# The 64 sample rows' projections and the gate rows computed on two column groups of the array

## The chip, the cores and the metric

The kernel runs on one Trainium2 chip, on all 8 cores, each with its own share of the batch. A core has a matrix engine (PE, the TensorE), a vector engine (DVE), a scalar engine (ACT), a general engine (POOL), a queue engine (SP) and 16 DMA engines. The time is that of the slowest of the 8 cores, in device microseconds (us). "Span" is what the profile gives for one core, from its first to its last instruction; the time is some 1.6 us more than the longest span (1.5 to 1.7). A run is in a fast state or in a slow one, in which one die (cores 0 to 3, or 4 to 7) runs at a lower clock.

## The reference

One trunk layer. Each core has one prompt of 2048 tokens and 16 samples of 4 tokens, 64 sample rows in all, so 17 tiles of rows: 16 of 128 tokens, and tile 16 with the samples.

```python
mod = (silu(c) @ w_ada + b_ada)[:, None, :]
sh1, sc1, gt1, sh2, sc2, gt2 = split(mod, 6)            # shift, scale, gate, twice
h    = rmsnorm(x, g_pre_mix) * (1 + sc1) + sh1
proj = h @ w_in
mix  = concat([pool_mixer(...), conv_mixer(...)]) @ w_out     # "output projection"
x    = x + gt1 * rmsnorm(mix, g_post_mix)
h2   = rmsnorm(x, g_pre_ffn) * (1 + sc2) + sh2
up   = h2 @ ffn_w_up
a, b = split(causal_dwconv(concat([ffn_buf, up]), ffn_conv_w), 2)
f    = (silu(a) * b) @ ffn_w_down                              # "down projection"
x    = x + gt2 * rmsnorm(f, g_post_ffn)
# outputs: x, and the last rows of the pooling, convolution and FFN inputs
```

The model width is 1024 (`D`), the FFN width 2816. A gate (`gt1`, `gt2`) is one row for the prompt and one for each of the 16 samples.

## The kernel before

The program lists operations; a planner orders them on the engines by a simulated schedule and draws each dependency as a semaphore. So a change in one place can move the order of loads and of PE everywhere.

The gate rows are products with the stationary operand `REP`, the conditioning with each sample's column repeated for its 4 tokens, plus one for the prompt: 65 columns, one product for each half of the channels. They go through a DRAM scratch to be spread over partitions:

```python
def gate_rows(n, hb):                       # n: first or second gate, hb: half of the channels
    ib, ig = (0, 1) if n == 0 else (4, 5)   # buffers; BIG[4] is "big_79" in the profile
    ...
    mm(PSF[0:65, b, :], [(REP[:, kc, :], W[:, kc, :]) for kc in range(KC)], ..., 512)
    tt(rb[0:65, sl], PSF[0:65, b, :], rb[0:65, sl], ALU.add, ...)       # + bias
    tt(rb[0:65, sl], rb[0:65, sl], rg[0:65, sl], ALU.mult, ...)         # * post-norm weight
    if hb == 1:
        store(gsc_d[n], rb[0:65, :], [r_big[ib]], ...)                  # to the scratch
def gate_load(n):
    # GTS[0:64, :] <- rows of the samples; GTP <- the prompt's row, to 128 partitions
```

The output and down projections of a tile fill a pair of PSUM banks, one for each half of the channels; then the tail normalizes, gates and adds.

```python
def o_mm(t):                                # d_mm(t) is alike, with 22 products a half instead of 8
    b = tail_a(t, x_d, ())                  # takes a bank pair, loads x
    for hb in range(2):
        mm(PSF[0:rows, b + hb, :], [(BY[:, kc, r0:r0 + rows], WO[hb][:, kc, :]) for kc in range(KC)], ..., 512)
def tail_b(t, k, add_eng, parts=1):
    m = turn(tmps)                          # temporary; the first one is BIG[4]
    stats(ps, ...)                          # Square with sum into BIG[m] (as scrap), sqrt, reciprocal
    stt(BIG[m], ps, rstd, gt, mult, mult)   # * 1/rms * gate
    give(b, b + 1)                          # the banks are free
    tt(BIG[xi], BIG[m], BIG[xi], add)       # + x, then the store of y
```

For tile 16 only 64 of the 128 stationary columns are used.

## Time and profile before

| | us |
|---|---|
| time, median of fast runs | 744.4 (744.08 to 744.72) |
| spans of the 8 cores | 740.4 to 742.2 |
| PE busy, slowest core | 691.0 |
| gate rows, 4 groups of 8 products | 6.9 |
| samples' output projection, 16 products | 3.5 |
| samples' down projection, 44 products | 9.6 |
| end of PE to end of span, mean of cores | 5.9 |

From the page of the kernel before, the span, and the line of busy time (us, share of the span, instructions):

```profile
span 742.2 us, 12030 instructions; the slowest of 8 cores (740.4 to 742.2 us)
...
PE 691.0 (93%) x3925; PEld 332.7 (45%) x4000; DVE 469.2 (63%) x624; ACT 328.1 (44%) x576; POOL 271.4 (37%) x293
```

From here on, a line of a timeline has start, duration, engine, line of the kernel, operation, output and inputs, shapes and count; brackets at its end give how long the engine had been idle and what released it. The timeline of PE before, core 2, two of the four gate products:

```profile
164.44 1.89 PE L468 MATMUL ps<-ring_70,rep_46 128*65 128x512 bf16 x8
...
177.27 1.89 PE L468 MATMUL ps<-wg_73,rep_46 128*65 128x512 bf16 x8
```

Eight matmuls of 512 columns take 1.73 us from start to start, with 65 stationary columns as with 128. The timeline before, core 0, ACT at the first two output tiles:

```profile
192.92 1.02 ACT L489 ACTIVATE big_79<-ps 128x1024 bf16<-128x1024 f32 x1 [2.97 <-PE ps L468]
...
196.32 1.02 ACT L489 ACTIVATE big_80<-ps 128x1024 bf16<-128x1024 f32 x1 [1.90 <-PE ps L468]
```

The timeline before, core 2, the end of the kernel:

```profile
726.64 1.02 ACT L489 ACTIVATE big_80<-ps 64x1024 bf16<-64x1024 f32 x1 [8.06 <-PE ps L468]
726.65 9.44 PE L468 MATMUL ps<-wdn_134,g_135 128*128 128x512 bf16 x43 [0.16 <-issue]
...
729.95 1.22 DVE L497 TENSOR_TENSOR big_78<-big_80,big_78 64x1024 f32<-64x1024 f32 x1 [0.17 <-DVE big_80 L493]
...
736.19 0.60 ACT L489 ACTIVATE big_80<-ps 128x512 f32<-128x512 f32 x1 [4.01 <-PE ps L468]
```

The samples' tail (726.6 to 731.2) is hidden under the last tile's matmuls. After PE's end at 736.1 there is only the last tile's second half.

### The profile page before, as it was taken

To read this page: it belongs to the slowest core of one execution; us is meant where nothing else is said; L and a number is where in the kernel's file an instruction comes from. 1 tells how busy PE (TensorE), PEld (TensorE's weight loads), DVE (VectorE), ACT (ScalarE), POOL (GpSimd) and SP (SyncE) were. 2 spreads that over 40 slices of the span, in tenths; PEclk is the share of its full clock that TensorE was granted. 3 is DMA by queue.
4 is the path that set the end of the run, shared out by engine and by line. 5 is a ranking of instruction groups with operands and counts; after the bars stand their busy time and mean duration, and the time that the engine had idled before them with its cause. 6 is when DMAs were issued, how large, how long until landed. Compare 5 with 4: busy or idle time off the path is not lost.

```text
span 742.2 us, 12030 instructions; the slowest of 8 cores (740.4 to 742.2 us)
## 1 busy us (share of the span) xinstructions
PE 691.0 (93%) x3925; PEld 332.7 (45%) x4000; DVE 469.2 (63%) x624; ACT 328.1 (44%) x576; POOL 271.4 (37%) x293
## 2 busy tenths in 40 slices
PE   1588889999999999999999999999999999999996
PEld 1244435544455444444444444445444444444442
DVE  2348688745478889997777511128877777767213
ACT  4526754433477784454454311134444444423111
POOL 2313332232488653434444232223433342322320
PEclk9969999999999999999999999999999999999999
DMA  8999999599868554346989974113335433062422
GB/s 207 187 202 216 204 176 188 102 189 200 229 229 268 202 118 82 57 72 101 149 151 151 208 228 166 57 57 57 59 64 88 76 58 57 1 232 86 137 77 72
DMA packets 25713, 101.33 MB, mean 137 GB/s; under 512 B 3310, under 2 KB 5102, under 8 KB 21812
## 3 DMA queue, kind: packets, MB, share of 16 engines
q0 software_dynamic: 10944, 47.85, 39.8%
q1 hardware_dynamic: 14708, 52.71, 21.6%
q8 instruction: 33, 0.54, 0.3%
q14 instruction: 28, 0.23, 0.1%
HBM read 127.49 MB, written 20.90 MB: 200 GB/s over the span
## 4 chain that ended last, share of the span: by engine, by line
PE 84%; DVE 5%; issue 5%; DMA 3%; ACT 1%; POOL 1%; DVEq 0%; SPq 0%; ACTq 0%; POOLq 0%
PE ps L468 81%; PE ps L695 2%; DMA wsc_2_85<-w_sc 2%; PE ps L476 2%; DMA big_77<-x 1%; DVE big_75 L493 1%; DVE big_79 L493 1%; POOL big_77 L497 0%; DVE ta_107 L493 0%; DVE big_80 L493 0%; DVE ah_81 L502 0%; DVE ah_81 L504 0%; ACT ah_81 L489 0%; DVE by_82 L493 0%; DVE xn_99 L502 0%
## 5 line engine op out<-in xcount | busy, mean ns | idle before, releaser
L468 PE MATMUL ps<-wdn_134,g_135 128*128 128x512 bf16 (+1 forms) x733 | 161.4, 379 | 0.9 <-issue 0.2
L468 PE MATMUL ps<-ah_81,ring_71 128*128 128x512 bf16 (+2 forms) x766 | 148.5, 346 | 5.6 <-DVE ah_81 L502 2.2
L468 PE MATMUL ps<-ah_81,ring_72 128*128 128x512 bf16 (+2 forms) x798 | 148.4, 338 | 2.2 <-DVE big_75 L493 1.1
L468 PE MATMUL ps<-ah_81,ring_70 128*128 128x512 bf16 (+2 forms) x739 | 138.0, 339 | 3.2 <-DVE ah_81 L502 0.9
L468 PEld LDWEIGHTS ps<-wdn_134,g_135 128*128 128x128 bf16 (+1 forms) x748 | 73.3, 99 | 87.1 <-issue 0.8
L468 PEld LDWEIGHTS ps<-ah_81,ring_71 128*128 128x128 bf16 x784 | 67.8, 98 | 80.5 <-issue 6.8
L468 PEld LDWEIGHTS ps<-ah_81,ring_72 128*128 128x128 bf16 x816 | 68.8, 98 | 76.8 <-issue 2.4
L468 PEld LDWEIGHTS ps<-ah_81,ring_70 128*128 128x128 bf16 x752 | 63.6, 98 | 72.0 <-issue 3.6
L586 DVE RECIPROCAL stat_55<-stat_55 128x1 f32<-128x1 f32 (+1 forms) x67 | 10.6, 158 | 121.0 <-ACT stat_55 L489 120.7
L497 POOL TENSOR_TENSOR g_135<-big_75,big_76 128x1024 bf16<-128x1024 f32 x15 | 35.4, 2361 | 65.9 <-DVE big_76 L497 34.4
L497 POOL TENSOR_TENSOR g_135<-big_77,big_78 128x1024 bf16<-128x1024 f32 x15 | 35.4, 2357 | 58.0 <-DVE big_78 L497 32.7
L497 POOL TENSOR_TENSOR g_135<-big_79,big_80 128x1024 bf16<-128x1024 f32 x14 | 33.4, 2383 | 55.3 <-DVE big_80 L497 27.5
L489 ACT ACTIVATE big_80<-ps 128x1024 bf16<-128x1024 f32 (+2 forms) x16 | 15.5, 969 | 73.6 <-PE ps L468 72.7
L493 DVE SCALAR_TENSOR_TENSOR big_75<-ps,vecs_43,big_75 128x1023 f32<-128x1023 f32 (+1 forms) x30 | 38.4, 1278 | 11.8 <-ACT halob_58 L489 4.9
L493 DVE SCALAR_TENSOR_TENSOR big_77<-ps,vecs_43,big_77 128x1023 f32<-128x1023 f32 (+1 forms) x30 | 38.4, 1280 | 11.0 <-ACT halob_58 L489 6.2
L493 DVE SCALAR_TENSOR_TENSOR big_78<-ps,vecs_43,big_78 128x1023 f32<-128x1023 f32 (+1 forms) x30 | 38.4, 1279 | 10.4 <-ACT halo_57 L489 5.0
L493 DVE SCALAR_TENSOR_TENSOR big_76<-ps,vecs_43,big_76 128x1023 f32<-128x1023 f32 (+1 forms) x30 | 38.4, 1279 | 9.3 <-ACT halob_58 L489 4.4
L493 DVE SCALAR_TENSOR_TENSOR big_79<-ps,vecs_43,big_79 128x1023 f32<-128x1023 f32 (+1 forms) x28 | 35.8, 1280 | 12.3 <-ACT halob_58 L489 7.6
L493 DVE SCALAR_TENSOR_TENSOR big_80<-ps,vecs_43,big_80 128x1023 f32<-128x1023 f32 (+1 forms) x28 | 35.8, 1279 | 7.9 <-ACT halob_58 L489 3.6
L489 ACT ACTIVATE big_79<-ps 128x1024 bf16<-128x1024 f32 x14 | 14.3, 1023 | 55.8 <-PE ps L468 54.8
L497 POOL TENSOR_TENSOR big_75<-big_79,big_75 128x256 f32<-128x256 f32 (+1 forms) x16 | 20.0, 1250 | 49.6 <-DVE big_79 L493 30.9
L468 PE MATMUL ps<-wo_138,by_82 128*128 128x512 bf16 (+1 forms) x134 | 31.9, 379 | 0.1
(316 smaller groups left out, 895.2 us busy)
## 6 DMA issues: line engine op xcount, KB each, us to landing
ring_70<-w_up POOLq DMA_DIRECT2D x8, 1024.0 KB, 10.2
ring_71<-w_up POOLq DMA_DIRECT2D x7, 1024.0 KB, 10.9
ring_72<-w_up POOLq DMA_DIRECT2D x7, 1024.0 KB, 10.0
wdn_134<-w_down POOLq DMA_DIRECT2D x11, 512.0 KB, 13.9
y<-big_75 SPq DMA_DIRECT2D x7, 512.0 KB, 3.0
y<-big_76 SPq DMA_DIRECT2D x7, 512.0 KB, 2.6
y<-big_77 SPq DMA_DIRECT2D x7, 512.0 KB, 3.7
big_76<-x SPq DMA_DIRECT2D x6, 512.0 KB, 8.7
```

The source lines that it names most:

```text
L468: inst = e.matmul(bank_ap, l, r, start=(first and i == 0), stop=(last and i == len(pairs) - 1))
L476: inst = e.transpose(o, i, ident)
L489: return K.op("act", lambda e: e.activation(out=out, in_=in_, func=func, **kw), reads=reads, writes=writes, cost=c_act(n, ptr))
L493: return K.op(eng, lambda e: e.scalar_tensor_tensor(out, in0, s, in1, op0, op1), reads=reads, writes=writes, cost=c_dve(n))
L497: return K.op(eng, lambda e: e.tensor_tensor(out, in0, in1, op), reads=reads, writes=writes, cost=c_dve(n) if eng == "dve" else c_pool(n))
L586: K.op("dve", lambda e: e.reciprocal(STAT[0:rows, k + 1, t:t + 1], STAT[0:rows, k + 1, t:t + 1]), reads=[r_stat[k + 1][t]], writes=[r_stat ...
L695: inst = e.matmul(PSF[:, start_b[g, c], :], WINP[:, kc, g * 128:(g + 1) * 128], AH[:, kc, c * 512:(c + 1) * 512], start=(kc == 0), stop=(k ...
```

## The change

With 64 columns or fewer in the stationary operand, two products can use two halves of the array's columns: here the two halves of the channels. The samples' tile then has its channels folded over 128 partitions (64 rows times two halves of 512), so its vector work is half as long. The price: a row's sum of squares lies in two partitions, and a small fp32 matmul with a pairing matrix adds the two. The gate rows use 32 stationary columns (16 samples, prompt, padding), once for both halves.

```diff
+    def mm2(outs, ls, rs, reads, writes, n):
+        def fn(e):
+            for i in range(len(ls)):
+                for o, r in zip(outs, rs[i]):
+                    inst = e.matmul(o, ls[i], r, start=(i == 0), stop=(i == len(ls) - 1))
+    def stats2(src, k, reads, junk, junk_regs):
+        act(junk, src, AF.Square, ..., accum=STAT[:, k, 16:17])
+        mm(PSF[:, b, 0:1], [(PAIR, STAT[:, k, 16:17])], ...)            # adds the halves
+        act(STAT[:, k + 1, 16:17], PSF[:, b, 0:1], AF.Sqrt, ...)        # then reciprocal
-    def gate_rows(n, hb):
+    def gate_rows(n):                       # both halves at once
+        mm2([PSF[h * 32:(h + 1) * 32, b, :] for h in range(2)], [SC[:, kc, :] for kc in range(KC)],
+            [(W0[:, kc, :], W1[:, kc, :]) for kc in range(KC)], [r_sc] + r0 + r1, [r_bank[b]], 512)
-        K.dma("sp", ... GTS[0:TS, :] <- gsc_d[n, 0:TS, :], GTP <- gsc_d[n, TS:TS + 1, :] ...)   # 4 KB rows
+        K.dma("sp", ... GTP[:, h * 512:(h + 1) * 512] <- gsc_d[n, h, 0:1, :] for h in range(2)  # 2 KB rows
+              ... GTS[h * 64:(h + 1) * 64, :] <- gsc_d[n, h, 1:17, :] for h in range(2) ...)
-    todo = {(2, 4): [pool_states, lambda: gate_rows(0, 0), lambda: gate_weights(1, 1)],
-            (2, 0): [lambda: ada2(7), lambda: gate_rows(0, 1)],
+    todo = {(2, 4): [pool_states],
+            (2, 0): [lambda: ada2(7), lambda: gate_rows(0), lambda: gate_weights(1, 1)],
             (2, 1): [lambda: ada2(4), lambda: ada2(5), lambda: gate_load(0)],
-            (2, 3): [lambda: gate_rows(1, 0)], (3, 1): [lambda: gate_rows(1, 1)]}
+            (3, 1): [lambda: gate_rows(1)]}
     def o_mm(t):                            # and d_mm alike
+        if t == 16:
+            mm2([PSF[h * 64:(h + 1) * 64, b, :] for h in range(2)], [BY[:, kc, T:T + TS] for kc in range(KC)],
+                [(WO[0][:, kc, :], WO[1][:, kc, :]) for kc in range(KC)], ...)
+            return
# cut: tail_samples (the tail of tile 16 in the folded layout), turn_samples, loads and stores by halves
```

## The prediction

> **What bounds the kernel now.** The matrix engine (PE). The page has it busy 691 of 742 us; the chain of waits is 84% matmul. It idles in the first 110 us (table of stretches: 73 us busy of 110; start-up, DMA) and the last 6. From 110 to 240 us it is busy 128 of 130, from 325 to 736 nearly always. From 240 to 325 us VectorE is busy 78 of 85 us and PE idles 3.7: there VectorE limits.
>
> **Removed.** In the timeline a 512-column matmul takes 0.216 us start to start, with 128 stationary columns and with the samples' 64 alike. At least half of the array is idle or repeats rows in three places:
> - gate rows: 4 groups of 8 matmuls, 6.9 us, at 138 to 179 us;
> - samples' output projection: 16, 3.5 us, at 250 to 254 us;
> - samples' down projection: 44, 9.6 us, at 717 to 726 us.
>
> If two column groups stream at once, half of these 20 us goes: 3.45 + 1.7 + 4.75 = 9.9 us. The Trainium skill, "TensorE: Matmul & The Clock Gate", Part 3, states that such matmuls overlap (2.38x for three column tiles); "TensorEngine Tiling", Key Properties and Restrictions, that a change of mode drains the array and that column tiling has no fast weight load. This trace has no such pair. Loads of 64 columns take 110 ns and hide; two a pair should just fit. Gaps around the 64-column group are some 0.15 us; I take 0.5 us for all drains, and expect 9.0 to 9.4 us of PE.
>
> VectorE also loses four 0.69 us gate operations where it does not limit, and where it does, about 1.3 us on the samples' tile (1.27 to 0.7, 0.73 to 0.45, one PSUM copy moved to ScalarE).
>
> **Added.** Three one-column fp32 matmuls that add the halves' sums of squares, each between a square and a root. Two fall among the first up projections, where in-order PE may wait: up to 1 us. The third comes after the last tile's matmuls. Then the samples' root, reciprocal, scaling and addition (0.3 + 0.15 + 0.7 + 0.7), which before ran at 728 to 731 us under the last tile's matmuls, come after PE's end, mixed with the last tile's. I expect that tail, now 6 us, to grow by 1.6. A 64 KB load more: up to 0.4 us.
>
> **On the critical path.** Gates 3.1 us; output projection stage, VectorE's 1.3 less the small matmuls, 1.0; down projection 4.6; tail -1.6; start -0.1. Sum 7.0: 744.4 - 7.0 = **737.4 us**, range 734.5 to 741.0. Faster by over 2%: 0.02; within 2%: 0.96; slower: 0.02.
>
> **What would show it right.** The samples' down projection takes 4.8 to 5.2 us (over 8: the groups do not overlap). Each gate's 16 matmuls take some 1.8 us. From the samples' output projection to about 325 us PE idles 3 to 5 us. After the last 512-column matmul come one fp32 matmul and two VectorE operations of 128 by 512 for the samples, before the last tile's final scaling; PE end to span end is 7 to 8 us.
>
> **What would make it wrong.** No overlap of the groups: about 746. Weight loads of a pair that do not hide: half the gain. PE stalls at the small matmuls: 1 to 3 us less gain. The reordered, DMA-bound start moves by 1 to 2 us either way. A better scheduled tail: 736.

## More of the kernel before

Weights pass through a ring of three 1 MB slots. The third gate product reads slot 0, and the first load of the up projection takes that slot when the product is done.

The kernel is bound by PE, and its cores end together.

## The result, and the profile after

The kernel after took 745.31 us (median of 4 fast runs, 743.7 to 745.78), the kernel before 744.23 in the same rounds: ratio 1.001, 95% interval 0.9993 to 1.0027, the same. Ratios here are the mean time of one kernel's fast runs over that of the other's of the same rounds, so not quite the ratio of the medians that I quote. A later repetition gave 746.2 against 744.78, ratio 1.0028. The call "within 2%" held; the number, 737.4 with a range up to 741.0, did not.

The page after:

```profile
span 743.5 us, 12028 instructions; the slowest of 8 cores (733.4 to 743.5 us)
...
PE 681.7 (92%) x3926; PEld 328.2 (44%) x4002; DVE 464.0 (62%) x617; ACT 324.0 (44%) x575; POOL 269.5 (36%) x291
...
PE 75%; DMA 13%; DVE 4%; issue 4%; POOL 1%; ACT 1%; DVEq 0%; ACTq 0%; POOLq 0%; SPq 0%
```

PE is busy 9.3 us less on the two pages, as the prediction said (9.0 to 9.4). That difference is rough: both sums are of cores whose traces miss some 75 matmul records, and both hold matmuls at half clock; on the cores with all records PE is busy 692.4 to 696.1 us before and 683.2 to 685.8 after. The groups themselves bear the prediction out. From start to start, the gates' went from 6.9 to 3.7 us and the samples' down projection from 9.5 to 4.9; with some 1.7 of the output projection that is 9.5 us, less the small matmuls. But the chain that ended last now has 13% DMA, where before it had 3%, and the cores no longer end together. The view of all cores after:

```profile
core 0: 743.5 us, clock 0.986
core 1: 734.1 us, clock 0.991
core 2: 734.7 us, clock 0.991
core 3: 742.8 us, clock 0.989
...
core 7: 733.4 us, clock 0.991
```

Four of the eight cores are at 733.4 to 735.1 us, near the 735.2 that the prediction's 7 us would give from the span of 742.2; one is at 737.5 and three are at 743. The time is that of the slowest. From the start times of matmuls in each core's trace, the mean over cores of each stretch (and in brackets the least and the most where they differ much):

| stretch, us | before | after | change |
|---|---|---|---|
| start to first output-projection matmul | 188.7 | 185.3 | -3.4 |
| to the last output-projection matmul | 64.5 | 64.5 (61.8 to 70.4) | 0.0 (-2.7 to +5.9) |
| to the first down-projection matmul | 158.1 | 158.7 | +0.6 |
| to the end of PE | 324.2 | 319.6 | -4.6 |
| to the end of the span | 5.9 | 9.9 | +4.0 |
| span | 741.4 | 738.0 | -3.4 |

**The columns overlap.** The chain of waits after, core 0, at the second gate (start, us, what), and the start of the samples' down projection in the timeline after, core 7:

```profile
172.74 1.85 PE ps L480 x16
```

```profile
708.76 4.94 PE L480 MATMUL ps<-wdn_134,g_135 128*64 128x512 bf16 x44
...
713.63 9.67 PE L470 MATMUL ps<-wdn_134,g_135 128*128 128x512 bf16 x44
...
723.14 0.28 PE L470 MATMUL ps<-stat_55,pair_52 128*128 128x1 f32 x2
...
725.07 0.69 DVE L509 TENSOR_TENSOR big_78<-big_80,big_78 128x512 f32<-128x512 f32 x1 [0.17 <-DVE big_80 L505]
...
725.86 0.60 ACT L501 ACTIVATE big_80<-ps 128x512 f32<-128x512 f32 x1 [2.08 <-DVE big_78 L509]
...
727.69 0.60 ACT L501 ACTIVATE big_80<-ps 128x512 f32<-128x512 f32 x1 [1.14 <-DVE lastb_54 L516]
...
729.41 1.41 DVE L505 SCALAR_TENSOR_TENSOR big_75<-big_79,stat_55,big_75 128x512 f32<-128x512 f32 x2
```

The 44 matmuls take 4.87 us up to the next group's start, 0.221 us a pair, so two 64-column groups stream at the rate of one full matmul. The Trainium skill, "TensorE: Matmul & The Clock Gate", Part 3, gives 2.38x for three column groups of 32; two of 64, and two of 32 for the gates, here give 1.95 (4.87 us for 44 matmuls, where they took 9.5) and 1.88 (a gate's 16 take 1.84 us to the next group, not twice 1.73). Within a group the pairs follow every 0.216 us; the rest, some 0.11 us a group, lies at its ends. "TensorEngine Tiling", Key Properties, says that a change of mode drains the array: 4.87 less 22 times 0.216 leaves 0.12 us for both ends, whatever part of that is a drain.

**The tail** is in the same lines. The small fp32 matmul that joins the samples' sums comes behind all 44 matmuls of the last tile on PE, so the samples' root, scaling and addition begin at 723.4 and end at 725.8. The last tile's first square then waits 2.08 us for that addition (`big_78`), because its scrap buffer `big_80` is the samples' temporary. Before, both were under the matmuls. This is on every core: 9.9 us from the end of PE, 4.0 more.

**The stall.** The timeline after, core 0, ACT at the first output tile, then PE:

```profile
197.59 1.02 ACT L501 ACTIVATE big_79<-ps 128x1024 bf16<-128x1024 f32 x1 [11.90 <-DMA gate_scratch<-big_79]
```

```profile
200.89 3.57 PE L470 MATMUL ps<-wo_137,by_82 128*128 128x512 bf16 x8 [5.49 <-DVE stat_55 L595]
204.26 3.19 PE L470 MATMUL ps<-wo_138,by_82 128*128 128x512 bf16 x8
```

The first tile's temporary is `big_79`, the buffer that the second gate's rows are stored from, and that store has not landed. The Square waits 11.9 us; three tiles' bank pairs fill up and PE stops for 5.49 us. On this core it goes on at half clock: 8 matmuls in 3.57 and 3.19 us, not 1.89. The store took 20.7, 12.2, 11.7, 18.2, 12.0, 19.6, 17.1 and 12.6 us to land on cores 0 to 7; PE stopped on the four of over 17 us (0, 3, 5, 6; 1.8 to 5.5 us), and half clock followed on two of these (0 and 5). The chain of waits after, core 0, has that store as its longest piece:

```profile
176.77 20.73 DMA gate_scratch<-big_79
```

Why is it late? The issues of loads (POOL) and of the store (SP), before and then after, core 0:

```profile
166.82 0.57 POOL L508 DMA_DIRECT2D ring_70<-w_up  x1
...
181.08 0.33 SPq L512 DMA_DIRECT2D gate_scratch<-big_79  x1
```

```profile
175.12 0.57 POOL L520 DMA_DIRECT2D ring_70<-w_up  x1 [0.28 <-issue]
...
176.77 1.58 SPq L524 DMA_DIRECT2D gate_scratch<-big_79  x1
```

The 1 MB load for the up projection that goes to slot 0 ("the up load" from here on) is now asked for 1.65 us ahead of the store, not 14 us. I had two candidates: **A**, this load; **B**, that the rows of the first gate are now fetched in 384 pieces of 2 KB, not 192 of 4 KB, in the queue in which the store stands. Counted from the trace's packets, core 0 after, in 160 to 164 us: the load queue moved 65 packets of 8 KB, SP's queue 69 of 4 KB. They take turns by packet (as "DMA: Bandwidth & Descriptors", Queues, rings and completion order, says), so smaller packets mean fewer bytes for SP's queue as long as the other is busy. The 2 KB rows show it: on core 1 after, in 168 to 172 us, SP's queue moved 53 packets of 2 KB, 109 KB, beside 60 of 8 KB, 492 KB.

**The start.** PE is through the first shift products 2.7 us earlier (75.8 for 78.5, mean of cores), but only 0.6 us of it is left at the first product of the second modulation (122.3 for 122.8). The timeline of ACT, core 1, before and after; then PE after:

```profile
79.76 1.05 ACT L489 ACTIVATE xn_100<-big_79 128x1024 bf16<-128x1024 f32 x1
```

```profile
81.88 1.06 ACT L501 ACTIVATE xn_100<-big_79 128x1024 bf16<-128x1024 f32 x1 [4.62 <-DMA big_79<-x]
```

```profile
83.97 1.01 PE L488 MATMUL ps<-idb_51,xn_99 128*128 128x128 bf16 x8 [3.71 <-ACT ta_106 L501]
...
85.92 3.57 PE L470 MATMUL ps<-ah_81,ring_71 128*128 128x512 bf16 x8 [0.24 <-DVE ah_81 L638]
```

The x tile read there lands at 82.4 us (mean of cores) after and 79.7 before. Before, ACT came for it when it had landed, without a wait on seven of eight cores, by 0.1 to 4.8 us; after, ACT comes first and waits 3.0 to 4.6 us on all eight, PE idles, and 3.4 to 6.8 us at half clock follow.

### The profile page after: what moved, and what is told of

The parts are those of the page before. It is cut to its first block, busy times and chain, and to the rows that moved or that the text cites. A ratio compares the mean times of both kernels' runs of the same rounds, so it can differ in the third digit from the quotient of the medians.

```text
span 743.5 us, 12028 instructions; the slowest of 8 cores (733.4 to 743.5 us)
## 1 busy us (share of the span) xinstructions
PE 681.7 (92%) x3926; PEld 328.2 (44%) x4002; DVE 464.0 (62%) x617; ACT 324.0 (44%) x575; POOL 269.5 (36%) x291
## 4 chain that ended last, share of the span: by engine, by line
PE 75%; DMA 13%; DVE 4%; issue 4%; POOL 1%; ACT 1%; DVEq 0%; ACTq 0%; POOLq 0%; SPq 0%
PE ps L470 73%; DMA gate_scratch<-big_79 3%; DMA big_79<-x 2%; DMA big_78<-x 1%; DMA wsc_1_84<-w_sc 1%; DMA wsh_2_93<-w_sh 1%; DMA wsc_0_83<-w_sc 1%; DMA big_76<-x 1%; DMA ring_70<-w_inp 1%; PE ps L480 1%; PE ps L488 1%; DMA wsc_3_86<-w_sc 1%; DVE big_79 L505 1%; POOL big_78 L509 0%; DVE big_75 L505 0%
## 5 line engine op out<-in xcount | busy, mean ns | idle before, releaser
L470 PE MATMUL ps<-wdn_134,g_135 128*128 128x512 bf16 x689 | 151.8, 379 | 0.9 <-issue 0.2
L470 PEld LDWEIGHTS ps<-wdn_134,g_135 128*128 128x128 bf16 x704 | 68.5, 98 | 82.3 <-issue 0.4
L470 PEld LDWEIGHTS ps<-ah_81,ring_71 128*128 128x128 bf16 x784 | 67.8, 98 | 81.6 <-issue 7.9
L470 PEld LDWEIGHTS ps<-ah_81,ring_72 128*128 128x128 bf16 x816 | 68.9, 98 | 76.0 <-issue 1.3
L470 PEld LDWEIGHTS ps<-ah_81,ring_70 128*128 128x128 bf16 x752 | 63.7, 98 | 73.4 <-issue 4.7
L470 PE MATMUL ps<-wo_137,by_82 128*128 128x512 bf16 x125 | 31.6, 395 | 5.7 <-DVE stat_55 L595 5.5
```

Source lines behind the costliest of these rows:

```text
L470: inst = e.matmul(bank_ap, l, r, start=(first and i == 0), stop=(last and i == len(pairs) - 1))
```

## The experiments

All outputs were correct. "Stall" is PE's idle at about 200 us. The kernels of x5 to x8, and later x9 to x12, ran on a chip whose cores 4 to 7 were slow in every run; for these I give the mean over cores 0 to 3 of all timed runs (in the other rows, of the fast runs), where the kernel before has 742.5 (on the other chips it has 741.0 to 741.4).

| run | edit | time (fast), ratio to before | mean span of cores 0-3 |
|---|---|---|---|
| x1 | after, up load late | 740.7, 0.9944 (0.9926 to 0.9962) | 737.8 |
| x2 | after, other temporaries first | 743.0, 0.9979 (0.996 to 0.9997) | 737.4 |
| x3 | after, 4 KB gate rows | 743.7, 0.9971 (0.9932 to 1.0011) | 736.5 |
| x4 | after, samples' last tail early | 741.6, 0.9948 (0.9917 to 0.9978) | 733.5 |
| x5, x15 | before, up load late | 745.0, 1.0005 (0.9989 to 1.0021) (x15) | 741.8 (x5), 741.4 |
| x6 | after, gates as before | slow die | 736.3 |
| x7, x9 | x1 + x4 | slow die | 732.1, 732.8 |
| x8 | x1 + x3 + x4 | slow die | 731.9 |
| x10, x16 | x9 + w_ss after the last x | 734.5, 0.9862 (0.9846 to 0.9877) (x16) | 730.3, 729.9 |
| x11, x18 | x6 + x4 | 736.6, 0.9893 (0.9869 to 0.9918) (x18) | 733.2, 731.3 |
| x12, x14 | before, up load late, half rows | 745.5, 1.0009 (0.9993 to 1.0025) (x14) | 741.7, 741.7 |
| x13 | after, again | 746.2, 1.0028 (1.0007 to 1.0049) | 739.8 |
| x17 | after, states' store late | 744.7, 0.9993 (0.9936 to 1.0051) | 737.5 |

### x1 to x4: one edit each to the kernel after

x1 holds the up load of slot 0 until the fourth output tile's products:

```diff
-        up_slot[gi, pb] = ring_load(wup_d[pb], KC * 512)
+        up_slot[gi, pb] = ring_load(wup_d[pb], KC * 512, deps=[o_op[3]] if (gi, pb) == (0, 0) else ())
```

> The changed kernel with one load moved: the first up-projection weights into ring slot 0, which the merged gate rows now free just ahead of the second gate store, wait until the fourth output tile's matmuls are done. Theory A (that load, running on the DMA engines when the store of the second gate's rows is in the queue, delays the store's landing, and the first output tile's square, which reuses the store's buffer, waits for it): the store lands within about 10 us of its issue on every core instead of 12 to 21, PE does not stall before the fourth output tile on any core, the slowest core is near the fastest ones of the changed kernel, 733 to 737 us, and the time is 736 to 738 us against 744 before. Theory B (the halved rows double the packets of the gate loads in the same queue and hold the store up): the store still lands 12 us or more after its issue on some cores and the time stays at 742 to 746.

The store landed in 5.0 to 8.4 us on every core, and there was no stall on any. ACT in x1, core 0, at the first Square waits for PE alone again:

```profile
190.77 1.02 ACT L501 ACTIVATE big<-ps 128x1024 bf16<-128x1024 f32 x1 [2.95 <-PE ps L470]
```

The output stage took 61.8 us on every core. The time fell to 740.7, not to the 736 to 738 expected for this run, nor to the prediction's: the tail stayed, and the first output-projection matmul came 1.1 us later than in the kernel after (186.4 for 185.3, mean of cores), which I can't explain. What x1 moved is one load, from 175 to 201.5 us.

x2 keeps load and rows and takes temporaries that the store does not hold:

```diff
+    tmps[:] = [5, 4]                 # first output tiles
-            tmps[:] = [5, 8, 4]
+            tmps[:] = [8, 4, 5]
```

> The changed kernel with the temporary buffers of the output projection's tails taken in another order, so that the store's source buffer is first overwritten by the third tile, 6.9 us of matmuls later; loads and store are untouched. If the wait for the store's landing is what costs the time on the slow cores, the store still lands 12 to 21 us after its issue, but the stall of 2 to 6 us of PE and the half-clock matmuls after it go or shrink to under 2 us: slowest core 733 to 738 us, time 736 to 740. If the slow cores lose their time to something else (the start, the clock), 743 to 746 as the changed kernel.

That missed: the stall moved. The chain of waits of x2, core 1, and ACT there:

```profile
185.57 14.37 DMA ncp<-qlast
```

```profile
200.19 1.02 ACT L501 ACTIVATE e<-ps 128x1024 bf16<-128x1024 f32 x1 [9.18 <-DMA ncp<-qlast]
```

The next tile's temporary holds the source of the next store in the same queue, 4 KB, which took 14.4 us to land; PE stopped 2.3 to 3.8 us on four cores. So the queue is late as a whole, not this store.

x3 lays the scratch out so that the prompt's gate row is fetched as one 4 KB row again:

```diff
-    gsc_d = nc.dram_tensor("gate_scratch", [2, 2, 32, 512], F32, ...)
+    gsc_d = nc.dram_tensor("gate_scratch", [2, 32, 2, 512], F32, ...)
-              [e.dma_start(out=GTP[:, h * 512:(h + 1) * 512], in_=gsc_d[n, h, 0:1, :]...) for h in range(2)]
+              [e.dma_start(out=GTP, in_=gsc_d[n, 0:1].rearrange("r h f -> r (h f)")...)]
```

> The changed kernel with the scratch laid out so that the prompt's gate comes back in 128 rows of 4 KB in place of 256 of 2 KB; the ring load stays where the change put it. Theory B: 128 packets less ahead of the store bring its landing forward by 4 us or more, the stall shrinks from 6 us to under 2 on the slowest core, time 737 to 741. Theory A: the landing moves by 2 us or less, the time stays at 742 to 746.

That edit leaves 256 of the 384 pieces: 128 of 4 KB take the place of 256 of 2 KB. In the profiled run the store, now in two halves, had landed in 10.8 to 12.1 us on seven cores and in 18.9 on the one that stalled (core 3, 4.0 us). The timed runs, 740.0 to 745.1, are not clearly faster than before. With fewer and longer pieces fewer cores stalled, one of eight against four and six in the two profiles of the kernel after, but it is not a cure.

x4 moves the samples' last tail ahead of the second half of the last tile's products:

```diff
             for hb in range(2):
                 mm(PSF[0:rows, b + hb, :], ...)          # d_mm of tile 15
+                if t == 15 and hb == 0:
+                    tail_b(16, STFF, "dve")
```

> The changed kernel with the samples' small fp32 matmul of the down projection, and the samples' tail with it, put between the two halves of the last tile's matmuls. In the changed kernel's trace PE end to span end is 10.4 us against 6 before, because the last tile's squares wait for the samples' tail behind that matmul. Expected on every core: PE end to span end 6 to 6.5 us again, so 3.5 to 4.3 us less than the changed kernel, fastest cores at 729 to 731; the stall at the store is untouched, so the time is 741 to 742. If the tail is bound by something else (the last stores), it moves by under 1 us.

The timeline of x4, slowest core:

```profile
728.85 0.28 PE L470 MATMUL ps<-stat,pair 128*128 128x1 f32 x2
...
728.99 4.91 PE L470 MATMUL ps<-wdn,g 128*128 128x512 bf16 x22
...
731.57 0.60 ACT L501 ACTIVATE big<-ps 128x512 f32<-128x512 f32 x1 [2.08 <-DVE big L509]
```

The same wait of 2.08 us for the samples' addition is there, but under 22 matmuls. End of PE to end of span is 5.9 to 6.0 us on every core: the four lost microseconds were the order alone. Five cores still stalled (1.4 to 5.3 us).

### x5 to x8: the causes apart, the mends together

x5 is the kernel before with slot 0's up load held until the last gate product, so 1.5 us ahead of the store as in after (A without B):

```diff
-        up_slot[gi, pb] = ring_load(wup_d[pb], KC * 512)
+        up_slot[gi, pb] = ring_load(wup_d[pb], KC * 512, deps=[gate_op[1, 1]] if (gi, pb) == (0, 0) else ())
```

> The kernel before, with one edit: the same load of up-projection weights (ring slot 0) is held until the matmuls of the last gate group, where the changed kernel issues it, about 5 us ahead of the store of the second gate's rows. No column groups anywhere. Theory A (the load's time alone makes the stall): the store lands late, on some cores over 12 us after its issue, PE stalls 1 to 6 us at the third or fourth output tile on those cores, the slowest core gains 2 to 9 us: time 746 to 752. Theory B (the halved, doubled packets are needed for it): no core stalls, time 743.5 to 745.5, as before.

On cores 0 to 3 no stall, and 741.8 against 742.5: A alone does not make it, on this chip. One of the four, core 3, did wait 4.3 us for the store at its first Square (the others 3.0, for PE), but PE had enough ahead and did not stop. (x15 below repeats it.)

x6 is the kernel after with `gate_rows`, `REP`, the scratch and the `todo` list of before (`PAIR` moved to another free place):

```diff
-        mm2([PSF[h * 32:(h + 1) * 32, b, :] for h in range(2)], [SC[:, kc, :] ...], ...)
+        mm(PSF[0:65, b, :], [(REP[:, kc, :], W[:, kc, :]) for kc in range(KC)], ...)     # four groups, as before
```

> The changed kernel with the gate rows as they were (four groups of 8 matmuls, rows of 4 KB in the scratch, the ring slot free early); only the samples' output and down projections are merged. The ring load is then 14 us ahead of the store again. Theory A: no stall at the first output tiles on any core, all cores within the spread of the kernel before; against before the output stage gives 2.1 us, the down projection 4.6, the tail takes 4.1: 2.6 us, time 741 to 742.5. If the stall came from the other parts of the change, it is still there and the time is 744 or more.

No stall; 736.3 against 742.5, a gain of 6.2, well over what was expected. The start's 2.7 us earlier shift products are there too (76.2), so they come from the reordering, not from the gates.

x7 is x1 and x4 together, x8 adds x3.

> Both mends of the changed kernel: the ring load held until the fourth output tile, and the samples' small matmul between the halves of the last tile. The two are 550 us apart and should add up: no stall at the store on any core, PE end to span end 6 us, spans 729 to 735, time 736 to 738 (0.990 of before), against 741.1 with the first alone and 741.8 with the second alone. If it stays at 740 or more, the two share a cause.

> The two mends and the prompt's gate in rows of 4 KB. If packet count matters only by delaying the store behind a load, nothing is left to gain: within 1 us of the two mends alone, 735.5 to 738. If the short packets also slow other loads of that stage (x tiles, output weights), 1 to 2 us faster than the two mends alone.

x7: 732.1, no stall, tail 5.9, as expected on that die. x8: 731.9, so with the load out of the way, the size of the rows is worth nothing measurable.

### x9 to x12: again, and three finer questions

> The two mends together (first up load held back, the samples' last tail early), again, because their first run fell on a chip with one die in its slow state. On the undisturbed die it was 9.8 us under the kernel before. Expected in the fast state: 736 to 738.5 us, ratio to before 0.989 to 0.993, tail 5.9 us and no stall at the output projection on any core, 3 to 5 us of wait for the last x tile on ScalarE at about 82 us on every core, with the clock at half for 3.4 to 6.8 us after it. If the gain on the one die was luck of that chip, the ratio is 0.995 or more.

x9 is the kernel of x7. The same slow die fell to it. On the other die 732.8; the wait for the last x tile was 3.6 to 4.1 us on all four cores, as expected.

x10 holds the w_ss loads (weights of the second modulation, eight of 512 KB) until that x tile has landed; PE's order is unchanged:

```diff
-        load(W2[kc]..., wss_d[kc], [r_w2[kc]], 1 << 20, eng="pool")
+        load(W2[kc]..., wss_d[kc], [r_w2[kc]], 1 << 20, eng="pool", deps=[x_op[15]])
```

> As the run above, but the six half-megabyte and larger loads of the second modulation's weights wait until the x load of the last full tile has landed; order on TensorE unchanged. Theory: the 2.7 us that the new order gains at the start is swallowed at 82 us because that x load (512 KB, 12.5 to 14.8 us to land in the kernel after) shares the engines with these weights, and the 3 to 5 us gap then costs half clock as well. Then the load lands 3 us sooner or more, ScalarE waits under 2 us for it on most cores, the mean clock from 80 to 96 us is over 0.9, the first output projection comes 2 to 4 us earlier and the time is 733 to 735.5. Rival: this stretch is bound by bytes; the weights held back come late themselves and TensorE waits for them at 118 to 124 us, with no gain: within 1 us of the run above.

ACT at that tile, core 0, in x9 and in x10:

```profile
85.33 1.06 ACT L501 ACTIVATE xn<-big 128x1024 bf16<-128x1024 f32 x1 [3.57 <-DMA big<-x]
```

```profile
78.98 1.06 ACT L501 ACTIVATE xn<-big 128x1024 bf16<-128x1024 f32 x1 [1.59 <-DMA big<-x]
```

The waits were 1.6, 2.1, 3.1 and 2.3 us instead of 3.6 to 4.1; only one is under 2, and the clock from 80 to 96 us passed 0.9 on one core of four, so those details missed. But the first output-projection matmul came 2.5 us earlier (184.0 for 186.5) and the spans fell by 2.5, as expected. The rival, a stretch bound by bytes, falls.

x11 is x6 with x4's edit: gates apart, tail early.

> Gates as in the kernel before (four products with repeated conditioning), output and down projections of the samples merged, last tail early; up load as the schedule gives it. If merging the gates is worth the 3 us of TensorE time that it saves, this is 3 us over the first run of this call; if, as the runs so far say, the merged gates only shift a wait, it is within 1 us of it: 736 to 738.5 us, no stall at the output projection.

733.2 against x9's 732.8: merging the gates, with its stall mended, is worth 0.4 us (1.2 in the profiled runs), of some 3.2 saved on PE (four groups of 1.73 us against two of 1.84). Where the rest went is not shown. PE waits 2.30 us for DVE at about 100 to 105 us on all four cores of x9 and not in x11, but the kernel before has that wait too (2.2 us on all eight cores), so it does not come from the merged gates alone.

x12 is x5 with half rows too (A and B in the kernel before).

> The kernel before with two things from after alone: the first up load held until the last gate product, and the gate rows' loads cut into half rows (2 KB pieces, 384 instead of 192). Theory: late load and short pieces are both needed for the stall, so here the Square of the first output tile waits for the store of the second gate rows on at least 5 of 8 cores, by 2 us or more, TensorE loses 1 to 5 us on 3 or more of them, and the time is 1 to 4 us over before. Rival: something else of the merged gates (the earlier time at which the store is asked for, or the order on the queue) makes it: no wait for the store over 1 us on any core, time within 1 us of before.

One core of four waited for the store, by 0.4 us more than for PE; no stall. My theory, A and B together, missed. But the kernel after had not run on that chip, and the cores of the slow die ran out of step with the others (spans of 767 to 770 us beside 737 to 743).

### x13 to x18: the control, and what was open

Why the store is late was open. x13 is the kernel after unchanged, x14 is x12, x15 is x5, x16 is x10, all on one chip.

> The kernel after, unchanged, as a control. The runs that found no stall in the kernel before with the late load, and with late load and half rows together, fell on a chip whose other die was slow; the cores of a slow die run out of step and may leave the memory freer for the die that is measured. If the stall belongs to the kernel, the undisturbed cores here show it as at first: the Square of the first output tile waits for the store of the second gate rows on 5 or more of 8 cores (or 2 of 4), and TensorE loses 1.5 to 5.5 us on 2 or more of 8 (1 of 4). If it needs the load of all eight cores in step, the undisturbed die shows no stall here either and those two negative results say nothing.

> The kernel before with the late load and the half rows, again beside the kernel after. Theory (both are needed and enough): a wait for the store on about as many cores as in the run above. If the run above shows the wait and this one does not, late load and half rows are not enough, and what is left is how far the queue lags when the gate rows are asked for.

> The kernel before with the late load alone, again beside the kernel after. Theory: no wait for the store on any core, or on far fewer than in the run above; span within 1 us of before. Rival (late load alone is enough): waits as in the kernel after.

The kernel after stalled on six of eight cores, by 2.6 to 6.6 us. ACT and PE in x13, core 4:

```profile
197.76 1.02 ACT L501 ACTIVATE big<-ps 128x1024 bf16<-128x1024 f32 x1 [12.99 <-DMA gate_scratch<-big]
```

```profile
201.06 7.20 PE L470 MATMUL ps<-wo,by 128*128 128x512 bf16 x22 [6.58 <-DVE stat L595]
```

x14 waited for the store on two of eight cores, x15 on four. ACT and PE in x14, core 2:

```profile
195.80 1.02 ACT L489 ACTIVATE big<-ps 128x1024 bf16<-128x1024 f32 x1 [5.96 <-DMA gate_scratch<-big]
```

```profile
189.02 17.21 PE L468 MATMUL ps<-wo,by 128*128 128x512 bf16 x79
```

The waits were 3.1 to 6.0 us, where 2.9 is the ordinary wait for PE. PE ran through on every core. So A brings the store near the edge, but in the kernel before neither A nor A with B makes the stall: that part of my theory fell. Whether B adds to A is not clear from this: x15 waited on more cores, x14 longer. Nor does x14 rebuild the whole state of the queue. The first gate's rows, which stand ahead of the store, had landed 14 to 18 us after they were asked for in x14 and x15, and 24 to 27 us in the kernel after. What else differs is that PE in after reaches the output projection 3.4 us earlier, while the DMA work of the stretch is as large: from 160 to 190 us the share of the DMA engines is 1.00 before and 1.02 after (core 0). In x14 the store was in by 195.7 us at the latest; in x13's stalled cores it came at 197 to 198.5, and PE was ahead as well.

> The three mends together (first up load held back, samples' last tail early, second modulation's weights after the last x tile), for a verdict in the fast state. On the undisturbed die it was 729.9 us mean of the cores against 732.7 without the third mend and 742 before. Expected: 733 to 737 us, ratio 0.985 to 0.990.

x16: 734.51, ratio 0.9862, no stall, tail 5.9 on every core, as expected. It beats both kernels.

x17 is the kernel after with the 192 KB store of the samples' convolution states, which stands ahead of the gate rows' store in SP's queue, held until the fourth output tile:

```diff
-        store(ncs_d, QS.rearrange("p j s r -> p (j s r)"), [r_qs], nbytes=196608)
+        store(ncs_d, QS.rearrange("p j s r -> p (j s r)"), [r_qs], nbytes=196608, deps=[o_op[3]])
```

> The kernel after with one edit: the store of the samples' convolution states (192 KB in 1.5 KB pieces, asked for at about 167 us, ahead of the second gate rows' store in the same queue) waits until the fourth output tile's products. Up load, gate rows and the order on TensorE are as in the kernel after. Theory: the gate rows' store is late because it stands behind a backlog in its queue, whatever that backlog is made of; then its time to land falls from 18 to 22 us to 12 to 16 us, the stall on TensorE from 2.6 to 6.6 us to under 2 us on every core, and the time is 740 to 744 us. Rival: only the up load's place decides; then the landing stays over 17 us on most cores and the stall over 2 us on 4 or more.

The gate rows' store landed in 10.6 to 13.8 us on six cores and 16.6 and 19.0 on two; PE stopped on those two (1.5 and 3.9 us). So in this profile another part of the backlog, left out, goes the same way as the load left out, only less, and the rival (only the up load's place decides) falls. This is weaker than x1: one profiled run, while in one of the fast timed runs four cores were still at 742 to 747 us. "Under 2 us on every core" missed on one core, and the time, 739.9 to 748.1, is unclear. Landings here and in the kernel after fall into two groups, 10.6 to 14 and 16.6 to 21.8 us; what divides them I did not settle. The traces show two things that go with it, and no run moves either alone:

- *The rows ahead in the queue.* In after, x13, x2 and x4, 32 cores, the first gate's rows landed 4.8 to 7.6 us after the store was asked for on the 19 cores where the store took 15.7 us or more, and 1.3 to 4.2 us after it on the 13 where it took 13.9 or less. In x17, without the 192 KB, two cores with 4.8 and 5.1 us still landed in under 14.
- *Neighbouring cores.* In the 8 fast runs of the kernel after (result and x13), the cores of a pair (0 and 1, 2 and 3, and so on) differ in span by 4.1 to 13 us in 30 of 32 pairs; in those of the kernel before mostly by under 4. In all 16 pairs with one stalled core in the profiled runs, it is the core that asked for the store later. So nearly every pair has one late core, and the time is nearly always that of one. A profile of the slowest core alone does not tell that.

> Gates as in the kernel before, projections of the samples merged, last tail early, on a chip where the kernel after can be compared in the same state. Theory: with the gates apart the first up load stays early and the store lands in time, so no stall over 1.5 us on any core; the output projection begins at 186 to 188.5 us and the time is 737 to 740.5 us, so that merging the gates is worth at most 2 us even where its stall is mended (741.1 without the early tail, that is about 737 with it). Rival: the stall does not come from the merged gates; then 4 or more cores show it here too and the time is over 741.

x18 is x11: 736.62, just under what was expected, ratio 0.9893, no stall on any core. ACT at the first Square of x18 waits for PE alone, and PE runs through, core 0:

```profile
188.36 1.02 ACT L502 ACTIVATE big<-ps 128x1024 bf16<-128x1024 f32 x1 [2.90 <-PE ps L471]
```

```profile
184.65 17.43 PE L471 MATMUL ps<-wo,by 128*128 128x512 bf16 x79
```

The rival falls: the stall belongs to the merged gates. x4 is the same kernel but for the gates, their rows' layout in the scratch with them (and where the pairing matrix lies), and has 0.9948 in its rounds.

## Why the prediction was wrong

- **PE's saving (9.0 to 9.4 us): right.** 9.3 on the two pages, some 9.5 by the groups, less the small matmuls; a gate's group 1.85, the samples' down projection 4.9.
- **Down projection, -4.6: right.** 324.2 to 319.6 on every core.
- **"Gates 3.1 us; output projection stage ... 1.0": wrong, and the main failure.** The step that failed is the path: the prediction carried the gates' 3.1 us straight to the end, with DMA as hidden behind the output projection as before. The gates' stretch did become 2.8 us shorter (65.9 to 63.0), and PE came to the output projection 3.4 us earlier. But there the output stage, which was to give 1.0 more, took up to 5.9 us longer, because its first tile waited for a DMA. The chain: merging frees a ring slot some 8 us later, so a 1 MB load and the store of the gate rows meet in a stretch where the DMA engines are full, and the first output tile needs the store's buffer. On the late cores the store took 17 to 21 us to land. That stopped PE for 1.8 to 5.5 us on four of eight cores (x13: 2.6 to 6.6 on six), and half clock afterwards cost up to 3 us more on two of the four. x1 takes the load away, and the stall is gone; x18 takes the merged gates away, and it is gone. The kernel's time is its slowest core's, so three late cores cost the whole gain: mean span -3.4, slowest core +1.3.
- **"Start -0.1" and "the reordered, DMA-bound start moves by 1 to 2 us either way": half right.** PE gained 2.7 us there, and the wait for one x tile and half clock took most of it back on every core (0.6 left). x10 gets 2.5 us of it.
- **"Tail -1.6": the mechanism was right, the size was not.** It is 4.0. The prediction counted the samples' operations moved behind the end of PE, but not that the last tile's first square waits for them through the shared scrap buffer (2.08 us). x4 takes away all of it.
- **"PE idles 3 to 5 us" for VectorE in the output stage:** PE idles 2.8 to 3.3 us in after between the end of the output stage and 325 us, where before it was 3.2 to 3.9; the longest wait, 1.6 us, ends at 248 to 258 us; the stage is 2.7 us shorter where it does not stall, where I had 1.0 (x1: 61.8 for 64.5), and 0.6 of it is lost in the stretch after it.
- **"PE stalls at the small matmuls: 1 to 3 us less gain" among the risks:** not seen apart; the risk that came true, DMA between 160 and 200 us, is not in the list.

The sum with the mends: x16 saves 10.3 us by medians (744.78 to 734.51).

What stays open: which part of the backlog is the last straw for the store, why only one core of nearly every pair is late, and whether gates apart with x10's edit would do as well as x16.

## What to carry to other kernels

Side-by-side column groups give the factor of two on PE, but ask of each merged group what it holds longer: here merging two products delayed the release of a weight slot, and the load that was waiting for it met a store whose buffer the next stage needed. When PE is made faster in a stretch where DMA is full, look for the first buffer that PE then reaches too early, and in the tail, put a small matmul that other engines wait for ahead of the last long group. Look at all cores, not at the mean: one late core is the kernel's time.

## What the Trainium skill lacked or had wrong

- "TensorE: Matmul & The Clock Gate", Part 1, says that half clock comes after at least one idle window of some 3.4 us, which runs freely. The windows are right: the stretches at half clock here are 3.41, 6.83 or 13.65 us long. But the window need not be idle. (The page's section on PSUM-queue cycling does say that frequent short idles between groups can bring half clock back, but gives no busy share.) Laid on that grid, windows with PE busy 0.32, 0.33, 0.34 and 0.36 of the time were followed by half clock (gaps of 2.2 to 2.6 us), and windows with 0.44, 0.60, 0.64 and 0.70 were not; a gap of 2.96 us that lay across two windows (0.70 and 0.44, after, core 3) cost nothing. Laid over every core of twelve fast profiles, 144 of 144 windows begun at full clock with PE busy under 0.40 were followed by half clock, none of 622 above 0.46, and 5 of 23 between. So a gap of 2.2 us can cost some 1.7 us more by luck of its place (an estimate: half of a window of 3.41 us).
- The same page, Part 1, says to budget 13/16 clock for all-core dense matmul. In the fast state all eight cores run dense matmuls at a mean granted clock of 0.988 to 0.995 before. In the slow state the slow die's records do show stretches at 0.8125 of 5 to 14 us, with 0.95 as the mean (x9, core 5: 0.953).
- The same page, Part 3, has figures for three column groups of 32 but none for two. Here two groups of 64 columns take 0.221 us a pair at 512 columns, their 64-column weight loads hidden (44 in 4.46 us), and two groups of 32 take 1.85 us for 16.
- "DMA: Bandwidth & Descriptors" says that queues take turns by packet, but not what that means for a queue of short rows: SP's queue with 4 KB packets moved 283 KB in 4 us beside 532 KB of the queue with 8 KB packets, 69 packets against 65.
